# Values as seven products of quarters between the convolution's units, and attention in full f32

## The chip, the cores and the metric

The kernel runs on one core of one Trainium2 chip. The metric is the device time of one execution in microseconds (us). Three executions before the change took 316.39, 316.88 and 317.06 us, with a median of 316.88.

The core's engines work side by side, each through its own queue, in order: TensorE (PE) multiplies matrices, VectorE (DVE) and ScalarE (ACT) work element by element, GpSimd (POOL) does small things and issues some transfers, and SyncE (SP) issues most transfers.

## What is computed

One decoder layer on 256 tokens of width 1024, with two mixers that read the same modulated, normalised input `h`:

```python
proj = h @ w_in
q, k, v, g_attn, cb, cc, cx, g_conv, m_attn, m_conv = jnp.split(proj, IN_OFFSETS, axis=-1)
attn = moba_attention(split_heads(q), split_heads(k), split_heads(v), rel_bias)
y_attn = (attn * jax.nn.silu(g_attn)) @ w_o_attn
y_conv = (short_conv(cb, cc, cx, conv_w) * jax.nn.silu(g_conv)) @ w_o_conv
merged = jax.nn.sigmoid(m_attn) * y_attn + jax.nn.sigmoid(m_conv) * y_conv
return x + gate[:, None, :] * (merged @ w_out)
```

With 256 tokens there is one block of keys, so the attention is plain causal attention of 8 heads of 128 with a bias by distance. A final RMSNorm follows. All data are float32.

## The kernel before

**Two halves for one number.** PE is fast in a reduced-precision form of float32 (`F32R`). The kernel splits each operand into a high half in that form, made by ACT (`split`, L75), and a low half, the rest, made by DVE (L76). A product is then three: high by high, low by high, high by low. Full-f32 products are written with plain f32 operands and need no split.

**Stages.** The transposed normalised input lies in `xnT`. In the first stage Q and K are built up in all eight PSUM banks, over eight k-tiles (`passes`, L205), while the modulated input `H` is made in halves k-tile by k-tile; the full value of a k-tile, `hf`, stands in a small buffer of its own (`full_h`). Then `evac` copies the eight banks into `QK`; ACT and DVE share that, and the splits of the first two weights of the next stage stand between (`vsplit`).

**V** comes next, as one block: `rows_half` makes each 512-column half of V from two weight quarters of 512 x 512 for both halves of the tokens. With two halves of the width, two of the depth and two of the tokens that is eight blocks of twelve PE products (four k-tiles, three products each, 512 columns).

**Units.** Then come twelve units of the convolution mixer: for `j` in 0 to 3 a `cc`, a `cx` and a `cb` unit, after them four `gc` and four `ga` units (the SiLU gates). A unit (`unit`, L350) loads 1 MB of weights through SP, splits them and makes 256 columns of the projection: 16 products of 512 columns (L358) and 16 of 256 (L360), then a `fold` on ACT and DVE.

**Slots.** The attention of head pairs 0 to 3 is spread over numbered slots, one behind each unit: `att_prep` splits Q and K of the pair, `att_scores` (slots 0, 3, 6, 9) makes the scores and the softmax, `att_trans` (slots 3, 6, 9, 12) transposes the weights and splits them and V, `att_out` (slots 6, 9, 12, 13) multiplies. A pair's transposes thus stand three slots behind its scores. Behind each `cx` unit, `gate_part` reduces 1 MB of weights on DVE for the layer's gate.

**Seven products.** `mc` and `oc`, the merge gate's projection and the convolution's output projection, are already made by the class `Seven`: the 1024 x 1024 weight and the input are cut in quarters, and seven products of quarters with sums of quarters replace eight. The sums of weights are made by transfers that add into their target (`add_on`, on POOL's queue); the sums of inputs are made by `combos`, which adds the halves of its input back together and forms four differences in buffers of their own. `p1` to `p7` are the products, interleaved with `ga` and `ma` (`tile`) units.

**Order.** The order of each engine's queue is made at compile time by a scheduler, from the program's order and from when it reckons an instruction's inputs to be ready. Instructions in `pin(...)` keep the program's order among themselves. Buffers: raw weights go round in five 1 MB buffers, and the halves in three each. PSUM banks are handed out in a ring.

Of the kernel before, what the change touches and what calls it, by code (L numbers as in the profile page):

```python
# [17 lines left out]
P = 128  # L18
D = 1024
# [21 lines left out]
def layer_kernel(ctx: ExitStack, tc, x, c, vec, wp_all, slab_all, onehot, final_g, out):  # L41
# [9 lines left out]
    RAW_BUFS = 5  # L51
# [9 lines left out]
    def raw_tile(shape, name):  # L61
        return wp.tile(shape, F32, tag="raw", name=name, bufs=RAW_BUFS)
# [24 lines left out]
    csb, cs = wide[:, 0:D], wide[:, D:D + P]  # L87
# [182 lines left out]
    hfs[0] = tp.tile([P, S], F32, tag="low", name="hf0", bufs=4)  # L270
# [13 lines left out]
    pin(nc.gpsimd.dma_start(rvd, rv))  # L284

# [64 lines left out]
    def unit(key, rhs, dst):  # L350
        name = f"{key[0]}{key[1]}"
        raw = load(key, "w" + name).rearrange("p (k n) -> p k n", k=KT)
        hi, lo = split(raw, [P, KT, 256], name)
# [23 lines left out]
    def rows_half(blk, n, xs, ready=None):  # L377
        a = [bank(f"a{blk}{n}{t}") for t in range(2)]
        for kh in range(2):
            if ready:  # L380
                hi, lo = ready[kh]
            else:
                raw = load((blk, n, kh), f"w{blk}{n}{kh}").rearrange("p (k n) -> p k n", k=4)
                hi, lo = split(raw, [P, 4, 512], f"{blk}{n}{kh}")
            for t in range(2):
                rows_mm(a[t], xs, t, hi, lo, 4 * kh, slice(0, 512), kh == 0, kh == 1)
        return a

    for n in range(2):
        av = rows_half("v", n, H, None if n else v0)  # L390
        for t in range(2):
            nc.scalar.activation(V[:, t, 512 * n:512 * (n + 1)], av[t], AF.Copy)  # L392
# [8 lines left out]
    AT = big.tile([P, NH, S], F32, tag="AT", name="AT")  # L401
    softmax, weights = {}, {}

    AX = big.tile([P, 3, 1536], F32R, tag="GA", name="AX")

    def hi_lo(i, c0, w, a):

        return [AX[:, i, c0 + s * a * w:c0 + (s + 1) * a * w].rearrange("p (a w) -> p a w", a=a) for s in range(2)]

    def put_halves(dst, src):  # L410
        hi, lo = dst
        nc.scalar.activation(hi, src, AF.Copy)
        nc.vector.tensor_sub(lo, src, hi.bitcast(F32))
# [4 lines left out]
    def att_prep(i):  # L418
        qk = QK.rearrange("p (h a) b -> p h (a b)", a=2)[:, 2 * i:2 * i + 2, P:]
        put_halves(hi_lo(i % 2, 0, 3 * P, 2), qk)  # L420

    def att_scores(i):
        his, los = hi_lo(i % 2, 0, 3 * P, 2)
# [3 lines left out]
        for g in range(2):  # L427
            (qh, kh), (ql, kl) = ((t[:, g, 0:P], t[:, g, P:]) for t in (his, los))
            for j, (q, k) in enumerate(((qh, kh), (qh, kl), (ql, kh))):
                nc.tensor.matmul(pS[g][:, P:384], q, k, start=(j == 0), stop=(j == 2))  # L430
# [17 lines left out]
    def att_trans(i):  # L448
        put_halves(hi_lo(2, 0, S, 1), V[:, 0:1, 2 * i * P:2 * (i + 1) * P])
        ET = tp.tile([P, 2, P], F32, tag="ET", name=f"ET{i}", bufs=1)  # L450
        pT = [bank(f"pT{h}") for h in heads_of(i)]
        for g in range(2):
            for b in range(3):
                cols = slice(b * P, (b + 1) * P)
                nc.tensor.transpose(pT[g][:, cols], softmax[i][:, g, cols], ident)
        his, los = hi_lo(2, 2 * S, S, 2)
        for g in range(2):
            put_halves((his[:, g], los[:, g]), pT[g][:, 0:S])
            nc.scalar.activation(ET[:, g], pT[g][:, S:384], AF.Copy)
        weights[i] = ET  # L460

    def att_out(i):
        pO = bank(f"pO{i}")
        (vh, vl), (eh, el) = hi_lo(2, 0, S, 1), hi_lo(2, 2 * S, S, 2)
        for g in range(2):
            cols = slice(g * P, (g + 1) * P)
            for j, (v, e) in enumerate(((vh, eh), (vh, el), (vl, eh))):
                pin(nc.tensor.matmul(pO[:, g * S:(g + 1) * S], v[:, 0, cols], e[:, g], start=(g == j == 0),
                                     stop=False, skip_group_check=True))
        for g, h in enumerate(heads_of(i)):  # L470
            pin(nc.tensor.matmul(pO[:, g * S + P:(g + 1) * S], V[:, 1, h * P:(h + 1) * P], weights[i][:, g],
                                 start=False, stop=(g == 1), skip_group_check=True))
# [3 lines left out]
    slots = [[] for _ in range(14)]  # L476
# [9 lines left out]

    n = 0
    for j in range(4):
        cc = unit(("cc", j), H, tmp("cc", f"cc{j}"))
        run_slot(n)  # L490
        n += 1
        cx = unit(("cx", j), H, tmp("cx", f"cx{j}"))
        run_slot(n)
# [34 lines left out]

    def add_on(t, key):
        pin(nc.gpsimd.dma_start(t, wp_all[UNIT[key]], accum_op=ALU.add))  # L530

    def combos(x, name, tags):
# [21 lines left out]
        return {3: out[0], 1: out[1], 2: out[3], 4: out[4]}  # L554

    class Seven:
        def __init__(self, blk, x, sink, home):
            self.blk, self.x, self.sink, self.home = blk, x, sink, home
# [4 lines left out]
        def begin(self):  # L563
            self.sum = big.tile([P, 2048], F32, tag=self.home, name=self.blk + "sum")
# [3 lines left out]
        def begin_first(self):  # L568
            self.first = load(self.key(1, 2), self.blk + "t1")
            add_on(self.first, self.key(1, 1))  # L570

        def product(self, a, raw, name, start, s=0, t=0, kh=0):
            hi, lo = split(raw.rearrange("p (k n) -> p k n", k=4), [P, 4, 512], self.blk + name)
            for k in range(4):
                if s:
                    xh, xl = self.sx[s][:, k, 0:P], self.sx[s][:, k, P:]
                else:
                    xh = self.x[:, 4 * kh + k, t * P:(t + 1) * P]
                    xl = self.x[:, 4 * kh + k, S + t * P:S + (t + 1) * P]
                for i, (w, xp) in enumerate(((hi, xh), (lo, xh), (hi, xl))):  # L580
                    nc.tensor.matmul(a, xp, w[:, k], start=(start and k == i == 0), stop=(k == 3 and i == 2),  # L581
                                     skip_group_check=True)
# [324 lines left out]
```

## Time and profile before

| what | value |
|---|---|
| median of three executions | 316.88 us (316.39 to 317.06) |
| span of the profiled execution, first to last instruction | 314.8 us |
| mean granted PE clock | 0.999 |
| end of Q/K, start of V on PE | 58.32 us |
| start of the first `cc` unit | 80.10 us |
| start of the first `ga` unit | 181.49 us |
| start of the `oc` product p5 | 247.38 us |
| data moved by transfers | 81.13 MB, 258 GB/s over the span |

The profile gives the profiled execution's span and not its own total, so the span is set beside the median: 2.1 us lie outside it. Times in rows are from the start of the span. A row of the chain of waits gives start, duration, and what worked; the groups give busy time and the mean duration of one instruction; in the timeline a bracket at the end gives how long the engine had been idle and what ended that.

### The profile page before, as it was taken

Reading aid. Unit: us, or ns where it says so; the run is one execution under the profiler, and the core shown is the slowest. Engines: PE = TensorE matmul, PEld = TensorE weight load, DVE = VectorE, ACT = ScalarE, POOL = GpSimd, SP = SyncE. Lnnn points to the kernel's source line nnn. Section 1 sums busy time; section 2 is a strip of 40 time slices with the busy share of each in tenths; the row PEclk is TensorE's granted clock in tenths of the full one; section 3 lists DMA queues with packets and bytes.
Section 4 is the critical chain, followed back from the end, with each engine's and each line's share of the span. In section 5 each row is a group of like instructions: output and inputs, shape, how many; then the busy total and the mean of one; then the engine's idle time right before and its main releaser. Section 6 shows DMA issues by size and latency. Waiting matters only on the chain.

```text
span 314.8 us, 4582 instructions
## 1 busy us (share of the span) xinstructions
PE 306.3 (97%) x1766; PEld 270.2 (86%) x1766; DVE 263.6 (84%) x343; ACT 200.1 (64%) x287; POOL 13.9 (4%) x26
## 2 busy tenths in 40 slices
PE   7899999999999999999999999999999999999993
PEld 6899999888888989889899888888888888888882
DVE  3998995968597999698778878999998588999943
ACT  2765656954559595666967677688896645653421
POOL 3300000000000000020000100020001000000001
PEclk9999999999999999999999999999999999999999
DMA  7999999987667393959964795859969987730003
GB/s 265 414 410 409 406 414 416 403 348 290 254 239 286 134 327 131 372 147 228 304 232 134 269 244 188 322 129 275 314 232 298 391 280 287 250 131 0 0 2 133
DMA packets 15643, 81.13 MB, mean 258 GB/s; under 512 B 1686, under 2 KB 3206, under 8 KB 8454
## 3 DMA queue, kind: packets, MB, share of 16 engines
q1 hardware_dynamic: 12976, 70.59, 58.4%
q0 software_dynamic: 1328, 8.93, 12.7%
q10 hardware_dynamic: 1318, 1.33, 1.3%
q8 instruction: 14, 0.23, 0.3%
q14 instruction: 7, 0.06, 0.0%
HBM read 79.77 MB, written 1.06 MB: 257 GB/s over the span
## 4 chain that ended last, share of the span: by engine, by line
PE 95%; DMA 2%; DVE 1%; issue 1%; SPq 0%; POOLq 0%; POOL 0%; DVEq 0%
PE acc L205 15%; PE agc L358 5%; PE acb L358 5%; PE acx L358 5%; PE acc L358 5%; PE aga L358 5%; PE mcB L581 3%; PE ocB L581 3%; PE aga L360 2%; PE acb L360 2%; PE acx L360 2%; PE acc L360 2%; PE agc L360 2%; PE aoa L373 2%; PE aoa L374 2%; PE av L374 2%
## 5 line engine op out<-in xcount | busy, mean ns | idle before, releaser
L399 DVE CUSTOM_DVE_ANT_0 gate<-gate,wide,vT 128x1024 f32<-128x1024 f32 x8 | 10.1, 1278 | 0.3 <-DMA gate<-in_wp_dram 0.3
L168 DVE CUSTOM_DVE_ANT_0 ada<-ada,wide,msc 128x1024 f32<-128x1024 f32 x7 | 9.4, 1342 | 0.0
L168 DVE CUSTOM_DVE_ANT_0 ada<-ada,wide,vT 128x1024 f32<-128x1024 f32 x7 | 9.0, 1279 | 0.0
L441 ACT ACTIVATE L<-L,mx 128x128 f32<-128x128 f32 (+1 forms) x16 | 7.1, 443 | 1.2 <-DVE mx L439 1.2
L344 ACT ACTIVATE lowcx<-acx 128x256 f32<-128x256 f32 x8 | 3.0, 376 | 7.2 <-PE acx L360 7.2
L445 ACT ACTIVATE L<-L,rr 128x128 f32<-128x128 f32 (+1 forms) x16 | 5.9, 447 | 0.2 <-DVE rr L443 0.2
L392 ACT ACTIVATE V<-av 128x512 f32<-128x512 f32 x4 | 2.4, 599 | 5.4 <-PE av L375 5.4
L565 POOL DMA_DIRECT2D mcsum<-in_wp_dram x1 | 0.6, 581 | 116.3 <-DVE cx L345 116.3
L76 DVE TENSOR_TENSOR cb0l<-wcb,cb0h 128x2048 fp32r<-128x2048 f32 x1 | 2.3, 2293 | 3.6 <-ACT cb0h L75 3.6
L365 ACT ACTIVATE M<-pm 128x512 fp32r<-128x512 f32 x4 | 2.2, 595 | 4.4 <-PE pm L734 4.4
L76 DVE TENSOR_TENSOR ocp1l<-woc,ocp1h 128x2048 fp32r<-128x2048 f32 x1 | 2.3, 2293 | 3.1 <-ACT ocp1h L75 3.1
L148 PE MATMUL wt<-ones 128*128 128x128 f32 x18 | 3.8, 381 | 1.0 <-DVE ones L134 1.0
L437 DVE CUSTOM_DVE_ANT_0 L<-pS,BI 128x128 f32<-128x128 f32 (+1 forms) x16 | 4.7, 350 | 0.0
L499 DVE SCALAR_TENSOR_TENSOR y<-cc,vT,y 128x255 f32<-128x255 f32 x8 | 3.5, 481 | 1.4 <-ACT y L498 1.4
L344 ACT ACTIVATE lowgc<-agc 128x256 f32<-128x256 f32 x8 | 3.0, 373 | 2.7 <-PE agc L360 2.7
L721 DVE TENSOR_TENSOR wo<-wo,gf 128x2048 f32<-128x2048 f32 x2 | 4.6, 2283 | 0.0
L344 ACT ACTIVATE lowcc<-acc 128x256 f32<-128x256 f32 x8 | 3.0, 371 | 2.3 <-PE acc L360 2.3
L172 ACT ACTIVATE H<-xnT,scs 128x256 fp32r<-128x256 f32 x7 | 4.1, 592 | 0.3 <-DVE scs L168 0.3
L76 DVE TENSOR_TENSOR cc0l<-wcc,cc0h 128x2048 fp32r<-128x2048 f32 x1 | 2.3, 2291 | 2.4 <-ACT cc0h L75 2.4
L148 PEld LDWEIGHTS wt<-ones 128*128 128x128 f32 x18 | 3.4, 284 | 1.0 <-DVE ones L134 1.0
L193 ACT ACTIVATE slab3h<-slab 128x1024 fp32r<-128x1024 f32 x2 | 2.1, 1061 | 3.3 <-DMA slab<-in_slab_dram 3.3
L443 DVE RECIPROCAL rr<-mx 128x4 f32<-128x4 f32 x4 | 0.7, 176 | 4.2 <-ACT L L441 4.2
(548 smaller groups left out, 1119.2 us busy)
## 6 DMA issues: line engine op xcount, KB each, us to landing
ada<-in_wp_dram SPq DMA_DIRECT2D x16, 512.0 KB, 10.3
slab<-in_slab_dram SPq DMA_DIRECT2D x16, 512.0 KB, 10.3
wv<-in_wp_dram SPq DMA_DIRECT2D x4, 1024.0 KB, 11.7
wcc<-in_wp_dram SPq DMA_DIRECT2D x4, 1024.0 KB, 4.9
wcx<-in_wp_dram SPq DMA_DIRECT2D x4, 1024.0 KB, 5.2
gate<-in_wp_dram SPq DMA_DIRECT2D x4, 1024.0 KB, 7.0
wcb<-in_wp_dram SPq DMA_DIRECT2D x4, 1024.0 KB, 6.3
wgc<-in_wp_dram SPq DMA_DIRECT2D x4, 1024.0 KB, 9.0
```

Source lines behind the costliest of these rows:

```text
L76: pin(nc.vector.tensor_sub(lo[:, s], raw[:, s], hi[:, s].bitcast(F32)))
L148: pin(nc.tensor.matmul(wt[:, 0:P], ones, ones, start=True, stop=True))
L168: pin(nc.vector.tensor_tensor_reduce(src, src, csb, vT[:, i:i + 1] if s else 1.0, bias(i, s), ALU.mult, ALU.add, scs[:, i, s:s + 1]))
L205: pin(nc.tensor.matmul(acc[j // 2][:, (j % 2) * S:(j % 2 + 1) * S], w[i][:, j * P:(j + 1) * P], x, start=(i == 0 and j // 2 not in opened) ...
L344: nc.scalar.activation(low, a[:, S:], AF.Copy)
L358: nc.tensor.matmul(a, hi[:, k, cols], rhs[:, k, :], start=(k == 0), stop=False)
L360: nc.tensor.matmul(a[:, S:], lo[:, k, cols], rhs[:, k, 0:S], start=False, stop=(k == KT - 1))
L373: nc.tensor.matmul(a, xh, hi[:, k4, cols], start=(first and k4 == 0), stop=False, skip_group_check=True)
L374: nc.tensor.matmul(a, xh, lo[:, k4, cols], start=False, stop=False, skip_group_check=True)
L399: nc.vector.tensor_tensor_reduce(src, src, csb, 1.0, vT[:, 24 + d:25 + d], ALU.mult, ALU.add, gcol[:, d:d + 1])
L441: nc.scalar.activation(E[:, g, cols], E[:, g, cols], AF.Exp, bias=mx[:, 4 + j:5 + j], accum_out=mx[:, 8 + j:9 + j])
L581: nc.tensor.matmul(a, xp, w[:, k], start=(start and k == i == 0), stop=(k == 3 and i == 2), skip_group_check=True)
```

## The change

1. The eight blocks of V become seven products `v1` to `v7`, in the manner of `Seven`. They no longer stand as a block: behind the units of slots 1 to 6 stand v1; v5; v3; v6; v7 and v2; v4. They use PSUM banks 5 to 7, and the units and the attention of that time the other five.
2. The full value of each k-tile of the modulated input is now written back into `xnT`, so that `combine(xnT)` can form the four differences in place, on DVE, ahead of the first eviction of Q/K. `combo_halves` splits them into halves, once for V and once more for `mc`; the `combos` of `H` is gone. The two splits between the evictions are now those of the first `cc` and `cx` units.
3. V's sums of weights: one addition on DVE, and three adding transfers on POOL's queue.
4. The attention products that were split in halves are now full f32: per head one 256-column score product in place of three, one 256-column output product in place of three. `att_prep` and the splits of the softmax weights and of V are gone, the transposed weights are copied whole by ACT.
5. The attention moves: scores of pairs 0 to 3 to slots 4, 7, 9, 11, transposes to 6, 8, 10, 12, output products to 8, 9, 11, 13. The four gate reductions move to the last two `cx` and the last two `gc` units.
6. Buffers: five named raw buffers; one holds the attention's bias, and one is held from v3 to v7. `Seven` gets its tiles from outside; the first of the `mc` and `oc` sums is now loaded on POOL's queue too, and `oc`'s takes the place of two `mc` combinations. `mc`'s p3 and p4 change places. The vector for the reductions and the products' spare buffers share one tile (`quads`).

The core of the diff:

```diff
     def full_h(i):
-        hfs[i] = tp.tile([P, S], F32, tag="low", name=f"hf{i}", bufs=4)
+        hfs[i] = xnT[:, i, :]
         modulated(i, hfs[i])
...
-    v0 = []
+    def quarter(f, t, kh):
+        return f[:, 4 * kh:4 * kh + 4, t * P:(t + 1) * P]
+
+    def combine(f):
+        f00, f01, f10, f11 = (quarter(f, t, kh) for t in range(2) for kh in range(2))
+        pin(nc.vector.tensor_sub(f11, f10, f11))
+        pin(nc.vector.tensor_sub(f10, f00, f10))
+        pin(nc.vector.tensor_sub(f00, f11, f00))
+        pin(nc.vector.tensor_add(f01, f00, f01))
...
+    combine(xnT)
+    vsum = big.tile([P, 2048], F32, tag="W2", name="vsum")
     for j in range(NT // 2):
-        if j < 2:
-            evac(j, j == 0)
-            v0.append(vsplit(j))
-        else:
-            evac(j, j % 2 == 1)
-    BI = big.tile([P, NH, 256], F32, tag="BI", name="BI")
+        evac(j, j in (0, 3, 5, 7))
+        if j == 0:
+            first_split(0)
+        elif j == 1:
+            first_split(1)
+    raw = load(("v", 0, 0), "wv11")
+    nc.sync.dma_start(vsum, wp_all[UNIT["v", 1, 0]])
+    first_v = {"vp1": split(raw.rearrange("p (k n) -> p k n", k=4), [P, 4, 512], "vp1", 1, pin)}
+    VX = big.tile([P, 4, 4, S], F32R, tag="GA", name="VX")
+    vsx = combo_halves(xnT, [(1, VX[:, 0])], pin)
+    pin(nc.vector.tensor_add(vsum, vsum, raw))
+    raw_ring.remove(4)
+    BI = raw_tile([P, NH, 256], "BI", 4)
...
-    for n in range(2):
-        av = rows_half("v", n, H, None if n else v0)
-        for t in range(2):
-            nc.scalar.activation(V[:, t, 512 * n:512 * (n + 1)], av[t], AF.Copy)
+    def v1():
+        product(vb[0], None, "vp1", own(H, 0, 0), True)
+        nc.scalar.activation(VQ[:, 1], vb[0], AF.Copy)
+
+    def v5():
+        product(vb[2], vsum, "vp5", vsx[1], True)
+        nc.scalar.activation(VQ[:, 0], vb[2], AF.Copy)
+        add_on(vsum, ("v", 1, 1))
+        vsx.update(combo_halves(xnT, [(4, VX[:, 1])]))
...
+    def v6():
+        product(vb[1], vsum, "vp6", vsx[2], True)
+        add_on(vsum, ("v", 0, 1))
+        nc.vector.tensor_add(VQ[:, 2], vb[1], VQ[:, 1])
+        nc.vector.tensor_sub(VQ[:, 0], VQ[:, 0], VQ[:, 1])
+        nc.vector.tensor_sub(v_at(0, 1), vb[2], VQ[:, 2])
+        vsx.update(combo_halves(xnT, [(3, VX[:, 3])]))
+
+    def v7():
+        product(vb[1], held["raw"], "vp7", vsx[3], False)
+        raw_ring.append(held["at"])
+        nc.vector.tensor_sub(v_at(1, 1), VQ[:, 0], vb[1])
+
+    def v2():
+        raw = load(("v", 0, 1), "wv21")
+        product(vb[0], raw, "vp2", own(H, 0, 1), False)
+        nc.scalar.activation(v_at(0, 0), vb[0], AF.Copy)
...
-        for g in range(2):
-            (qh, kh), (ql, kl) = ((t[:, g, 0:P], t[:, g, P:]) for t in (his, los))
-            for j, (q, k) in enumerate(((qh, kh), (qh, kl), (ql, kh))):
-                nc.tensor.matmul(pS[g][:, P:384], q, k, start=(j == 0), stop=(j == 2))
+        for a, h in zip(pS, heads_of(i)):
+            nc.tensor.matmul(a[:, P:384], QK[:, 2 * h, P:], QK[:, 2 * h + 1, :], start=True, stop=True)
...
-        his, los = hi_lo(2, 2 * S, S, 2)
         for g in range(2):
-            put_halves((his[:, g], los[:, g]), pT[g][:, 0:S])
-            nc.scalar.activation(ET[:, g], pT[g][:, S:384], AF.Copy)
+            nc.scalar.activation(ET[:, g], pT[g][:, 0:384], AF.Copy)
...
-        slots[max(3 * i - 2, 0)].append((att_prep, i))
-        slots[3 * i].append((att_scores, i))
-        slots[3 * i + 3].append((att_trans, i))
-        slots[13 if 2 * i + 2 == NH else 3 * i + 6].append((att_out, i))
+        slots[(4, 7, 9, 11)[i]].append((att_scores, i))
+        slots[(6, 8, 10, 12)[i]].append((att_trans, i))
+        slots[(8, 9, 11, 13)[i]].append((att_out, i))
+    early = {1: [v1], 2: [v5], 3: [v3], 4: [v6], 5: [v7, v2], 6: [v4]}
...
-        gate_part(j)
+        if j in (2, 3):
+            gate_part({2: 0, 3: 1}[j])
...
-        def begin_first(self):
-            self.first = load(self.key(1, 2), self.blk + "t1")
+        def begin_first(self, t):
+            self.first = t
+            pin(nc.gpsimd.dma_start(t, wp_all[UNIT[self.key(1, 2)]]))
             add_on(self.first, self.key(1, 1))
...
     tile("ma", 0, 0)
+    mc.p3()
+    oc.begin_first(big.tile([P, 2 * D], F32, tag="V", name="ocfirst"))
+    tile("ma", 0, 1)
     mc.p4()
-    oc.begin_first()
-    tile("ma", 0, 1)
-    mc.p3()
+    raw_ring.remove("BI")
     oc.sx = combos(GC, "c", ("W2", "BI"))
```

More of the change, by code (lines that the diff above doesn't have):

```diff
@@ L351, in unit @@
         name = f"{key[0]}{key[1]}"
-        raw = load(key, "w" + name).rearrange("p (k n) -> p k n", k=KT)
-        hi, lo = split(raw, [P, KT, 256], name)
+        if first:
+            hi, lo = first.pop(0)
+        else:
+            raw = load(key, "w" + name).rearrange("p (k n) -> p k n", k=KT)
+            hi, lo = split(raw, [P, KT, 256], name)
         for t in range(2):
@@ L389, in layer_kernel, with product @@
-    for n in range(2):
-        av = rows_half("v", n, H, None if n else v0)
-        for t in range(2):
-            nc.scalar.activation(V[:, t, 512 * n:512 * (n + 1)], av[t], AF.Copy)
+    def product(a, raw, name, xs, start):
+        hi, lo = first_v.get(name) or split(raw.rearrange("p (k n) -> p k n", k=4), [P, 4, 512], name)
+        for k in range(4):
+            xh, xl = (v[:, k, :] for v in xs)
+            for i, (w, xp) in enumerate(((hi, xh), (lo, xh), (hi, xl))):
+                nc.tensor.matmul(a, xp, w[:, k], start=(start and k == i == 0), stop=(k == 3 and i == 2),
+                                 skip_group_check=True)
@@ new lines, in layer_kernel, with v3 @@
+    held = {}
+    def v3():
+        held["raw"] = load(("v", 1, 1), "wv22")
+        held["at"] = raw_ring.pop()
+        product(vb[2], held["raw"], "vp3", vsx[4], False)
+        add_on(held["raw"], ("v", 1, 0))
+        vsx.update(combo_halves(xnT, [(2, VX[:, 2])]))
+    def v6():
[5 more added lines that the diff above has]
+        vsx.update(combo_halves(xnT, [(3, VX[:, 3])]))
@@ L485, in run_slot, with run_early @@
             f(h)
+    def run_early(i):
+        for f in early.get(i, ()):
+            f()
     n = 0
+    ring[:] = range(5)
+    turn[0] = 0
     for j in range(4):
+        if j == 3:
+            ring[:] = range(8)
+            turn[0] = 2
         cc = unit(("cc", j), H, tmp("cc", f"cc{j}"))
+        run_early(n)
+        if n == 6:
+            AT = big.tile([P, NH, S], F32, tag="AT", name="AT")
         run_slot(n)
@@ L553, in combos, with __init__, begin @@
         combo(4, nc.vector.tensor_add, v2, quarter(0, 1), "cx")
-        return {3: out[0], 1: out[1], 2: out[3], 4: out[4]}
+        return {s: (out[i][:, :, 0:P], out[i][:, :, P:]) for s, i in ((3, 0), (1, 1), (2, 3), (4, 4))}
+    turn3 = [0]
     class Seven:
-        def __init__(self, blk, x, sink, home):
-            self.blk, self.x, self.sink, self.home = blk, x, sink, home
+        def __init__(self, blk, x, sink):
+            self.blk, self.x, self.sink = blk, x, sink
         def key(self, r, c):
             return (self.blk, c - 1, r - 1)
-        def begin(self):
-            self.sum = big.tile([P, 2048], F32, tag=self.home, name=self.blk + "sum")
+        def begin(self, t):
+            self.sum = t
             pin(nc.gpsimd.dma_start(self.sum, wp_all[UNIT[self.key(1, 2)]]))
             add_on(self.sum, self.key(2, 2))
-        def begin_first(self):
-            self.first = load(self.key(1, 2), self.blk + "t1")
+        def begin_first(self, t):
+            self.first = t
+            pin(nc.gpsimd.dma_start(t, wp_all[UNIT[self.key(1, 2)]]))
             add_on(self.first, self.key(1, 1))
         def product(self, a, raw, name, start, s=0, t=0, kh=0):
[L573 to L582, printed above, removed]
+            product(a, raw, self.blk + name, self.sx[s] if s else own(self.x, t, kh), start)
         def quad(self, name):
-            return tp.tile([P, 512], F32, tag="q", name=self.blk + name, bufs=3)
+            turn3[0] += 1
+            c0 = turn3[0] % 3 * 512
+            return quads[:, c0:c0 + 512]
         def kept(self, a, name):
@@ L678, in layer_kernel @@
     mc.p5()
-    oc.begin()
+    raw_ring.append(mc.slot)
+    oc.begin(raw_tile([P, 2 * D], "ocsum", 4))
     gated("ga", AT, GA, 2)
```

121 lines of the change are left out of this document (66 added, 55 removed).

## The prediction

> **What bounds the kernel now.** I read the page's busy shares first, then the busy time by stage, then the chain that ended last, and went to the timeline only for single durations.
>
> ```profile
> PE 306.3 (97%) x1766; PEld 270.2 (86%) x1766; DVE 263.6 (84%) x343; ACT 200.1 (64%) x287; POOL 13.9 (4%) x26
> ```
> ```profile
> 58.32:80.10 21.78, 21.78 (x97) 18.01 (x97) 17.01 (x16) 11.76 (x12) 0.00 (x0) 1.00 0.86 342
> 80.10:156.04 75.94, 75.94 (x464) 67.93 (x463) 64.26 (x119) 54.66 (x112) 2.38 (x3) 1.00 0.70 240
> 156.04:181.49 25.45, 25.45 (x156) 22.73 (x156) 21.48 (x31) 18.27 (x30) 0.86 (x1) 1.00 0.63 212
> 181.49:247.38 65.89, 65.89 (x321) 55.70 (x321) 58.77 (x53) 49.88 (x54) 3.18 (x4) 1.00 0.84 258
> 247.38:307.50 60.12, 60.12 (x291) 50.48 (x290) 50.93 (x47) 29.91 (x29) 1.14 (x2) 1.00 0.42 153
> 99.00:117.00 18.00, 18.00 (x111) 16.12 (x110) 17.28 (x34) 13.73 (x31) 0.00 (x0) 1.00 0.56 200
> ```
> In each stage row the length stands first, then busy time of PE, weight loads, DVE, ACT and POOL, the granted clock, and the DMA share. In every stage the change can reach, PE's busy time equals the length, at a clock of 1.00: there is no bubble to remove, so only PE work taken away can shorten the kernel, and any late operand lengthens it at once. The last row shows how near the next engine is: DVE was busy 17.28 of 18.00 us there, and PE still did not wait.
>
> The span is 314.8 us and the median of the three times 316.88, so 2.1 us lie outside the span. The sum is made against the span and carried over to the median with that 2.1.
>
> **The change part by part.**
>
> *Values on PE.* The stage row 58.32:80.10 is the whole old V stage: 21.78 us for eight blocks of twelve 512-column products. The new V has seven.
>
> ```profile
> 239.22 2.72 PE ocB L581 x12
> 156.04 1.84 PE agc L358 x8
> 157.88 0.95 PE agc L360 x8
> 85.66 0.45 PE pS L426 x4
> 86.11 0.71 PE pS L430 x6
> 122.14 0.72 PE pO L468 x6
> 122.86 0.45 PE pO L471 x4
> ```
> These are rows of the chain: start, duration, work, count. A product of this form takes 2.72 us, so seven take 19.04 and **2.74 us go**. (One half of a unit is 1.84 + 0.95, so a unit is 5.58 us; I use that below.)
>
> *Attention on PE.* Per pair of heads the scores were 0.45 (two full-f32 128-column products, four records) + 0.71 (six reduced-precision 256-column products). The six become two full-f32 256-column products, that is four records. The only such form in the trace is the first block of Q/K:
>
> ```profile
> 11.40 3.72 PE L205 MATMUL acc<-hf,slab 128*128 128x256 f32 x16
> 14.78 2.26 PE L205 MATMUL acc<-H,slab0h 128*128 128x256 f32 x16
> ```
> Sixteen records fill 11.40 to 14.78: 0.211 us each. Four make 0.84, so scores gain 0.13 us; in the output product 0.72 becomes 0.84, plus 0.12. Four pairs: **+1.0 us**. Bounds: if 256 columns cost twice the 128-column record of 0.1125 (0.45/4), four make 0.90 and the sum is +1.5; downwards I allow a record of 0.20, since PE may have paused once in that stretch, which gives +0.7. I take 1.0, the row of the same form. The transposes stay as they are. Net on PE: 1.0 - 2.74 = **-1.74 us** (-1.2 to -2.0).
>
> The Trainium skill, "FP8 and Floating Point Precision", section "TensorE Precision Notes", says that true FP32 takes four passes through the array. By four passes of 0.118 the attention would cost +1.9 us and not 1.0; the row above, 0.42 us for a 256-column product, is below four times 0.118 = 0.47.
>
> *Where Q/K hands over.* The four in-place combinations are queued on DVE ahead of the first eviction.
>
> ```profile
> 50.94 1.23 DVE L200 TENSOR_TENSOR slab7l<-slab,slab7h 128x1024 fp32r<-128x1024 f32 x1 [0.40 <-ACT slab7h L193]
> 54.75 0.69 DVE L324 TENSOR_SCALAR QK<-acc 128x512 f32<-128x512 f32 x1 [2.59 <-PE acc L205]
> 58.15 0.40 PE L373 MATMUL av<-v00h,H 128*128 128x512 f32 x1
> ```
> DVE was idle 2.59 us before that eviction. Four operations of 128x512 (0.69 by the eviction's row, 0.60 apart when queued) take 2.4 to 2.8, so the eviction slips 0.2 us at most. PE wants that bank at 58.15, with 2.7 us to spare: cost 0. The two splits behind it are those that stood there before, of other weights.
>
> *DVE in the V window.* This is the cover that could run out. The old V ran as one block in which DVE was 17.01 of 21.78 busy; the new one stands between seven units and one pair of scores, 7 x 5.58 + 7 x 2.72 + 1.29 = 59.4 us of PE.
>
> ```profile
> L76 DVE TENSOR_TENSOR cb0l<-wcb,cb0h 128x2048 fp32r<-128x2048 f32 x1 | 2.3, 2293 | 3.6 <-ACT cb0h L75 3.6
> L366 DVE TENSOR_TENSOR GC<-sgc,GC 128x512 fp32r<-128x512 f32 x4 | 2.7, 687 | 0.0
> L345 DVE TENSOR_TENSOR gc<-agc,lowgc 128x256 f32<-128x256 f32 x8 | 3.3, 417 | 0.0
> L499 DVE SCALAR_TENSOR_TENSOR y<-cc,vT,y 128x255 f32<-128x255 f32 x8 | 3.5, 481 | 1.4 <-ACT y L498 1.4
> L437 DVE CUSTOM_DVE_ANT_0 L<-pS,BI 128x128 f32<-128x128 f32 (+1 forms) x16 | 4.7, 350 | 0.0
> ```
> DVE must do seven units at 2.29 + 2 x 0.42 (21.9), seven product splits (16.0), the sum of two weight quarters (2.3), four low halves and five value sums at 0.69 (6.2), two rounds of the convolution at 2 x 0.69 + 4 x 0.48 (6.6), the first scores (4 x 0.35 and two small ones, some 1.8), and three evictions (2.1), less the first split, done before 58.3: some 54.6 of 59.4, or 92%. The gate reductions leave this window, which makes it fit. At 96% PE did not wait in the row 99.00:117.00, so I put this at 0; the place most at risk is slot 5, where two products stand side by side (5.44 us of PE) just behind scores. Bound: 0 to 3 us, about one split and its queue. Over the stretch up to the gates' end DVE loses the halves of Q, K, E and V and the sum and differences of H, and gains splits: nearly even.
>
> *Transfers.* Three accumulating loads of V and the first load of the two "first" sums move to POOL's queue, which is nearly empty. Of the V ones each follows a product's split and is used two slots later: at least two units and a product, 13.9 us, lie between, against some 9 for the transfer and 4 for the split. The tight one is that of `oc`: it used to be loaded by SP long ahead; now its tile is the place that the `mc` combinations leave, so it waits for p3, which is moved to p4's old place.
>
> ```profile
> 222.90 2.72 PE mcB L581 x12
> 247.38 2.72 PE ocC L581 x12
> 258.26 2.72 PE ocB L581 x12
> ```
> ```profile
> 198.43 0.57 POOL L565 DMA_DIRECT2D ocsum<-in_wp_dram  x1 [18.05 <-PE mcC L581]
> 207.25 0.86 POOL L530 DMA_DIRECT2D ocsum<-in_wp_dram  x1 [8.25 <-DMA ocsum<-in_wp_dram]
> 207.94 1.06 POOL L530 DMA_DIRECT2D oct<-in_wp_dram  x1
> 239.31 1.92 ACT L75 ACTIVATE ocp5h<-oct 128x2048 fp32r<-128x2048 f32 x1 [1.92 <-PE ama L375]
> ```
> ```profile
> ocsum<-in_wp_dram POOLq DMA_DIRECT2D x3, 1024.0 KB, 8.9
> oct<-in_wp_dram POOLq DMA_DIRECT2D x1, 1024.0 KB, 15.7
> ```
> p3 ends at 225.62 - 1.74 = 223.9. The plain load takes 0.57 + 8.25, the accumulating one 8.9 from issue, so it lands at 241.6; ACT's half of the split (1.92) and DVE's (2.29) end at 245.8. PE wants the low half at 247.38 - 1.74 + 0.23 = 245.9. Nothing is left over for a busy ACT or DVE: I cost **+0.4 us** (0 if both are free, 2 if each is in the middle of a split). Behind it on POOL stands the next accumulation into the `oc` sum. Two accumulations that were queued together landed 207.94 + 15.7 - (207.25 + 8.9) = 7.5 us apart, so this one lands near 249.1 and is split by 253.3, ahead of p6 at 258.26 - 1.74 = 256.5.
>
> The Trainium skill, "DMA: Bandwidth & Descriptors", section "Anatomy of one DMA — SWDGE (gpsimd) path", gives 2.0 us plus bytes at 436 GB/s, 4.4 us for 1 MB (an estimate from that page). The trace has 8.25 and 8.9; by the page's figure this wait would be 0.
>
> *Raw buffers.* One of five goes to the bias for the attention's length, and one is held between v3 and v7. SP waited for buffers before without PE noticing; cost 0, bound 1 us.
>
> **Sum:** -1.74 + 0.4 = **-1.3 us**, 315.6.
>
> **The rivals.**
>
> *1. The transposes wait for softmax (slower).* Scores used to stand three slots ahead of their transposes. Now for pairs 1, 2 and 3 what stands between is 5.58 + 1.29, 5.58 and 5.58 us.
>
> ```profile
> 124.41 0.71 PE pS L430 x6
> 133.13 1.49 ACT L445 ACTIVATE L<-L,rr 128x128 f32<-128x128 f32 x4
> 144.15 0.71 PE pS L430 x6
> 152.63 1.48 ACT L445 ACTIVATE L<-L,rr 128x128 f32<-128x128 f32 x4
> ```
> Softmax took 134.6 - 125.1 = 9.5 and 154.1 - 144.9 = 9.2 us. If PE's queue holds program order, it stands for 2.6 + 3.8 + 3.8 = 10 us and the time is 326. From a wait of 1.3 us in all it eats the gain, so an eighth of this is enough to decide. For it: nothing else hides a transpose at the head of PE's queue. Against it: the order on each engine is made by readiness, and PE's queue shows it where a sum was late:
>
> ```profile
> 275.83 1.28 DVE L708 TENSOR_TENSOR SA<-SA,SC 128x512 f32<-128x512 f32 x2
> 276.46 0.40 PE L373 MATMUL aoa<-oa10h,GA 128*128 128x512 f32 x1
> 276.69 0.38 PE L734 MATMUL pm<-ident,SA 128*128 128x128 f32 x2
> ```
> The transposes of the merged rows, written ahead of `oa10`, were put between its products, at the moment when DVE's first sum was ready, without idle PE. Also DVE and ACT have less to do around the scores than they had. I expect the same there; a partial miss of one third gives 319.
>
> *2. DVE starves PE in the V window.* Row for: 92% and two adjacent products; row against: 96% without a wait. Price 2 to 3 us, which gives 317.6 to 318.6.
>
> *3. Only the handovers cost.* The late `oc` sum at its bound of 2 us or a few small waits take 1.2 to 2 us of the 1.74: 316.3 to 317.2, no difference to be told.
>
> *4. Full f32 costs four reduced-precision products* (0.47 for 256 columns): +1.9 in place of +1.0, which gives 316.5. The first Q/K block speaks against it.
>
> *5. Nothing is late at all,* or the f32 record is at its lower bound: 314.9 to 315.2.
>
> **How the numbers follow.** Chances: forecast, with the V saving, 1.0 for attention and up to 0.8 of handover, 0.50 (315.2 to 316.2); case 5, 0.08; case 3, 0.16; case 4, 0.04; case 2, 0.08; case 1, 0.14. A measurement of this kernel tells about 0.2% (0.6 us) from no change, so faster is below 316.25: 0.50 + 0.08 = 0.58. Within 0.2%: 0.16 + 0.04 = 0.20. Slower: 0.08 + 0.14 = 0.22. The range reaches from 314.9 to 318.5, which leaves out most of case 1 and little else.
>
> **What would show it.** Right: seven runs of twelve products of 2.72 us; four records of about 0.21 us under the 256-column scores; PE's busy time about 304.6 with no idle time between Q/K and the end; transposes of pairs 1 to 3 standing inside the next unit. Wrong: idle PE ahead of a transpose with ACT's scaled copy as the releaser (case 1); idle PE ahead of v7, v2 or v4 released by a low half (case 2); idle PE ahead of the `oc` product p5 (case 3); records near 0.235 us (case 4). The prediction falls if the order of PE's queue doesn't follow readiness, or if the accumulating loads on POOL take much more than 9 us beside SP's.

## The result, and the profile after

The changed kernel takes **320.64 us** (median of five runs, 317.90 to 320.93) against 316.88 (316.39 to 317.21) before: ratio 1.0098, 95% interval [1.0071, 1.0125], so it is slower. Measured once more on another occasion it took 319.75 (six runs), ratio 1.0091 [1.0068, 1.0114]. The forecast was 315.6 with a range up to 318.5. The profiled execution took 320.76 us with a span of 318.7, so 2.1 us lie outside the span, as before.

First the page of the changed kernel: busy time of PE and the other engines, and the line of the clock granted to PE in 40 equal slices of the span (8 us each).

```profile
PE 309.3 (97%) x1738; PEld 270.5 (85%) x1738; DVE 268.2 (84%) x339; ACT 201.7 (63%) x277; POOL 17.7 (6%) x31
...
PEclk9999999999999999999999999999999799999999
```

PE has fewer instructions than before (1738 for 1766) and yet 3.0 us more busy time. One digit of the clock, the 32nd slice, is a 7. So part of the loss is not waiting but slow work, in one place. Where the time went is read from the starts of the first record of each stage in the timeline (us, the row of differences from the same instants of before):

| stage | before | changed | difference |
|---|---|---|---|
| start to first Q/K product | 11.40 | 11.84 | +0.4 |
| Q/K, V, attention, to `ga0` | 169.93 | 169.12 | -0.8 |
| `ga0` to the first record of `oc` p5 | 65.89 | 66.20 | +0.3 |
| p5 and `oa` 0 0, to p1 | 8.16 | 11.96 | **+3.8** |
| p1 to the end of the span | 59.42 | 59.58 | +0.2 |

The first row wanders: over the twelve profiles of this study it lies between 11.1 and 12.1. The gain of V and attention together, in the second row, is there (-0.8) but is half of the forecast -1.74, and one product, p5, gives back several times as much. This is the timeline of PE at p5 in the changed kernel; in brackets stands the idle time ahead and who ended it:

```profile
247.16 0.49 PE L429 MATMUL ocC<-ocp5h,sxcW 128*128 128x512 f32 x1
249.49 0.79 PE L429 MATMUL ocC<-ocp5l,sxcW 128*128 128x512 f32 x1 [1.83 <-DVE ocp5l L81]
250.08 1.05 PE L429 MATMUL ocC<-ocp5h,sxcW 128*128 128x512 f32 x2
250.93 0.63 PE L429 MATMUL ocC<-ocp5l,sxcW 128*128 128x512 f32 x1
251.36 1.05 PE L429 MATMUL ocC<-ocp5h,sxcW 128*128 128x512 f32 x2
252.21 0.63 PE L429 MATMUL ocC<-ocp5l,sxcW 128*128 128x512 f32 x1
252.64 0.75 PE L429 MATMUL ocC<-ocp5h,sxcW 128*128 128x512 f32 x2
253.23 0.39 PE L429 MATMUL ocC<-ocp5l,sxcW 128*128 128x512 f32 x1
253.46 0.39 PE L429 MATMUL ocC<-ocp5h,sxcW 128*128 128x512 f32 x1
```

Twelve records of this product take 2.72 us, 0.227 each, when nothing is late. Here the second came 2.33 us after the first, 2.1 late; and the eleven from 249.49 on took until 253.68, 4.19 us in place of 2.50: another 1.7. Together they are the +3.8. The stages by window (length, then busy time of PE, weight loads, DVE, ACT and POOL, granted clock, DMA share, and last the GB/s moved) put the 1.7 on the clock:

```profile
181.00:247.00 66.00, 66.00 (x322) 55.57 (x320) 53.47 (x50) 46.52 (x51) 3.72 (x5) 1.00 0.75 231
247.00:256.00 9.00, 7.11 (x24) 5.47 (x24) 7.03 (x4) 7.07 (x7) 0.56 (x1) 0.81 1.02 358
256.00:307.00 51.00, 51.00 (x245) 42.73 (x244) 47.69 (x41) 24.42 (x22) 0.00 (x0) 1.00 0.40 151
```
```profile
249.48:252.89 3.41, 3.40 (x8) 2.73 (x9) 2.93 (x2) 2.68 (x3) 0.56 (x1) 0.50 0.94 328
```
The last row is the stretch of the fall by itself: the clock was at half for 3.41 us, which is 1.7 us of PE work lost.

What was late is read backwards along the queues. POOL, ACT and DVE, from their timelines, then SP's loads beside them and the landing of the accumulating load (the last number of its row in the view of DMA issues):

```profile
225.64 0.57 POOL L647 DMA_DIRECT2D ocfirst<-in_wp_dram  x1 [17.31 <-PE mcC L429]
232.03 0.85 POOL L293 DMA_DIRECT2D ocfirst<-in_wp_dram  x1 [5.82 <-DMA ocfirst<-in_wp_dram]
237.07 0.87 POOL L293 DMA_DIRECT2D ocsum<-in_wp_dram  x1 [4.19 <-DMA woa<-in_wp_dram]
```
```profile
245.19 1.92 ACT L80 ACTIVATE ocp5h<-ocfirst 128x2048 fp32r<-128x2048 f32 x1 [8.61 <-DMA ocfirst<-in_wp_dram]
```
```profile
247.14 2.29 DVE L81 TENSOR_TENSOR ocp5l<-ocfirst,ocp5h 128x2048 fp32r<-128x2048 f32 x1 [7.55 <-ACT ocp5h L80]
```
```profile
223.15 9.42 SPq L71 DMA_DIRECT2D woa<-in_wp_dram  x2
234.01 5.97 SPq L71 DMA_DIRECT2D woc<-in_wp_dram  x2
```
```profile
ocfirst<-in_wp_dram POOLq DMA_DIRECT2D x1, 1024.0 KB, 13.1
```

The plain load of `ocfirst` was issued at 225.64 when p3 released the place, 1.7 us later than the 223.9 of the working. It landed sooner than reckoned, so the accumulating one was issued at 232.03, 0.7 us ahead of the working's 232.7. But the accumulating load landed 13.1 us after its issue and not 8.9. ACT stood idle 8.61 us for it and DVE 7.55; both were free, the data were not there. SP issued three loads of 1 MB in those 13 us: at 232.24 and 239.65, the second of each group (start plus length, less the 0.33 of the last issue), and at 234.01.

### The profile page after: what moved, and what is told of

Its sections match the earlier page's. It is cut to its first block, busy times and chain, and to the rows that moved or that the text cites. A ratio compares the mean times of both kernels' runs of the same rounds, so it can differ in the third digit from the quotient of the medians.

```text
span 318.7 us, 4512 instructions
## 1 busy us (share of the span) xinstructions
PE 309.3 (97%) x1738; PEld 270.5 (85%) x1738; DVE 268.2 (84%) x339; ACT 201.7 (63%) x277; POOL 17.7 (6%) x31
## 3 DMA queue, kind: packets, MB, share of 16 engines
q0 software_dynamic: 2048, 14.17, 19.5%
## 4 chain that ended last, share of the span: by engine, by line
PE 83%; DMA 6%; issue 4%; ACT 2%; DVE 2%; POOL 1%; POOLq 0%; DVEq 0%; ACTq 0%
PE acc L211 15%; PE acc L405 5%; PE agc L405 5%; PE acx L405 5%; PE aga L405 5%; DMA ocfirst<-in_wp_dram 4%; PE acb L405 3%; PE acc L407 2%; PE aga L407 2%; PE agc L407 2%; PE aoa L422 2%; PE aoa L421 2%; PE aoa L420 2%; PE ocC L429 2%; DMA gate<-in_wp_dram 2%
## 5 line engine op out<-in xcount | busy, mean ns | idle before, releaser
L487 DVE CUSTOM_DVE_ANT_0 gate<-gate,quads,vT 128x1024 f32<-128x1024 f32 x8 | 10.1, 1277 | 1.8 <-DMA gate<-in_wp_dram 1.8
L174 DVE CUSTOM_DVE_ANT_0 ada<-ada,quads,msc 128x1024 f32<-128x1024 f32 x7 | 9.4, 1342 | 0.0
L174 DVE CUSTOM_DVE_ANT_0 ada<-ada,quads,vT 128x1024 f32<-128x1024 f32 x7 | 9.0, 1281 | 0.0
L81 DVE TENSOR_TENSOR ocp5l<-ocfirst,ocp5h 128x2048 fp32r<-128x2048 f32 x1 | 2.3, 2292 | 7.6 <-ACT ocp5h L80 7.6
L574 ACT ACTIVATE y<-cc,vT 128x256 f32<-128x256 f32 x8 | 3.7, 500 | 2.1 <-DVE cc L570 2.1
L405 PE MATMUL agc<-H,gc1h 128*128 128x512 f32 x16 | 4.8, 413 | 0.0
L388 ACT ACTIVATE lowcb<-acb 128x256 f32<-128x256 f32 x8 | 2.9, 367 | 2.5 <-PE acb L407 2.5
L405 PE MATMUL acb<-H,cb3h 128*128 128x512 f32 x16 | 4.3, 403 | 0.0
L178 ACT ACTIVATE xnT<-xnT,scs 128x256 f32<-128x256 f32 x7 | 4.2, 599 | 0.2
L405 PE MATMUL acc<-H,cc2h 128*128 128x512 f32 x16 | 4.1, 401 | 0.2 <-ACT cc2h L80 0.2
```

Of the source, the lines that this page charges most:

```text
L174: pin(nc.vector.tensor_tensor_reduce(src, src, csb, vT[:, i:i + 1] if s else 1.0, bias(i, s), ALU.mult, ALU.add, scs[:, i, s:s + 1]))
L178: pin(nc.scalar.activation(dst, xnT[:, i, :], AF.Identity, scale=scs[:, i, 1:2], bias=scs[:, i, 0:1]))
L388: nc.scalar.activation(low, a[:, S:], AF.Copy)
L405: nc.tensor.matmul(a, hi[:, k, cols], rhs[:, k, :], start=(k == 0), stop=False)
L487: nc.vector.tensor_tensor_reduce(src, src, csb, 1.0, vT[:, 24 + d:25 + d], ALU.mult, ALU.add, gcol[:, d:d + 1])
```

## The experiments

In the text, *stretch* is the time from the first Q/K product to `ga0`, read as in the table (before 169.93, changed 169.12), and *p5 to p1* the fourth row of it (8.16 and 11.96).

**1. p3 earlier.** The load for p5 is released a tile of 5.4 us earlier.

```
     mc.p2()
-    tile("ma", 0, 0)
     mc.p3()
     oc.begin_first(big.tile([P, 2 * D], F32, tag="V", name="ocfirst"))
+    tile("ma", 0, 0)
     tile("ma", 0, 1)
```

> mc's p3 and the two loads of the oc first sum stand ahead of the first ma unit, so both loads start 5.4 us earlier; no other change. Theory A (the late oc first sum costs some 3.8 us at p5: a wait of 2.1 for its low half and 1.7 of products at a lower clock behind it): PE does not wait at p5, its clock stays 1.00, and the time falls by 3 to 4 us to about 317. Theory B (the loss is spread: full-f32 products and a fuller DVE in the V window): the time stays within 1 us of 320.6.

317.39 us (ten runs), ratio to before 1.0013 [0.9992, 1.0034]. From POOL's timeline and PE's waits in this kernel:

```profile
227.89 0.85 POOL L293 DMA_DIRECT2D ocfirst<-in_wp_dram  x1 [5.38 <-DMA ocfirst<-in_wp_dram]
```
```profile
PE agc L405 <- DVE gc L389: 1.6, 1, 1.6
PE wt L154 <- DVE ones L140: 1.0, 1, 1.0
PE acc L405 <- ACT cc2h L80: 0.4, 1, 0.4
PE ama L421 <- DVE ma10l L81: 0.2, 1, 0.2
```

The load landed 10.9 us after its issue, before PE wanted it; no row of p5 is left among the waits and p5 to p1 is 8.16 again. Between 2.4 and 3.3 us are back (against 319.75 and 320.64), so the late operand at p5 is where the loss was. Smaller waits remain; the profiled execution took 319.0 us, 1.6 more than the median, so its wait of 1.6 us at `gc` is probably not in the median.

**2. The second sum left out.** Another accumulating load stands on POOL's queue right behind. It goes, for `oc`.

```
         def p7(self):
...
-            add_on(self.sum, self.key(1, 1))
+            if self.blk != "oc":
+                add_on(self.sum, self.key(1, 1))
```

> The accumulation into the oc sum behind p7 is left out, so p6 of oc works with one weight quarter too few. It is the transfer that is issued 5 us after the late accumulation of the oc first sum. If the two share the queue's rate, the first sum lands 8 to 9 us after its issue and not 13.1, the wait at p5 falls from 2.1 us to 0 to 0.5 and the time by 2 to 4 us. If SP's two loads of 1 MB beside it are what slows it, it still takes 12 us or more and the time stays.

319.72 us, ratio 1.0088 [1.0056, 1.0120]. The load and the wait are as they were:

```profile
ocfirst<-in_wp_dram POOLq DMA_DIRECT2D x1, 1024.0 KB, 12.7
```
```profile
PE ocC L429 <- DVE ocp5l L81: 1.7, 1, 1.7
```

The load behind it on the same queue is not what slows it: without it 0.4 us less of 13.1.

**3. SP's loads left out.** On the changed kernel, all of SP's weight loads for `oc` and `oa` are left out; the loads of `wo` are tied to places that come free late, so that they do not move up into the gap.

```
-        raw = load((blk, n, kh), f"w{blk}{n}{kh}").rearrange("p (k n) -> p k n", k=4)
+        if blk == "oa":
+            raw = GA[:, 0:4, :].bitcast(F32)
+        else:
+            raw = load((blk, n, kh), f"w{blk}{n}{kh}").rearrange("p (k n) -> p k n", k=4)
...
         def load(self, r, c):
+            if self.blk == "oc":
+                return GA[:, 0:4, :].bitcast(F32).rearrange("p k n -> p (k n)")
...
+    raw_ring[:] = [4, "BI"]
```

> The changed kernel with all of SP's weight loads of oc and oa left out (their products read the tile GA in place of the weights, so the outputs are not the reference's), so that nothing of SP's moves beside the accumulating load for oc p5. Theory A (the accumulating load shares the DMA engines with SP's loads, which took it from 8.9 to 13 us): it lands 8 to 9 us after its issue, PE has no wait at p5, and the time is 2 to 4 us below the changed kernel: 316.5 to 318.5. Rival (an accumulating load queued behind a plain one with the second sum behind it takes 13 us by itself): it still takes over 12 us and PE waits 1.8 us as before.

316.49 us, ratio to before 0.9987 [0.9974, 0.9999], 3.3 us under the changed kernel's second measurement and 4.2 under its first. Landing, and ACT's half of the split:

```profile
ocfirst<-in_wp_dram POOLq DMA_DIRECT2D x1, 1024.0 KB, 7.9
```
```profile
238.47 1.92 ACT L80 ACTIVATE ocp5h<-ocfirst 128x2048 fp32r<-128x2048 f32 x1 [2.65 <-DMA ocfirst<-in_wp_dram]
```

With nothing of SP's beside it, and with the second sum still behind it, the same load on the same queue lands in 7.9 us: SP's loads beside it are the cause, shown from both sides. PE has no wait after the first Q/K product, and p5 to p1 is 8.16. The Trainium skill, "DMA: Bandwidth & Descriptors", section "Queues, rings and completion order", says that each DMA engine takes turns between the queues that have work, a packet at a time; 7.9 us alone and 13 beside SP agree with that. The fit in its section "Anatomy of one DMA — SWDGE (gpsimd) path", 4.4 us for 1 MB by an estimate from it, is below both.

**4. The wait filled.** Nine full-f32 products of the constant `ones` into the bank of p5, ahead of it, which p5's own first product clears.

```
         def p5(self):
             self.c = bank(self.blk + "C", 2)
+            if self.blk == "oc":
+                for _ in range(9):
+                    nc.tensor.matmul(self.c[:, 0:P], ones, ones, start=True, stop=True)
```

> Nine idle full-f32 products of two constant 128x128 tiles (2.0 us of PE) stand ahead of oc's p5, in the bank that p5 then opens. If the wait of 2 us alone lowered the clock behind it, the products of p5 come every 0.23 us again, and the time falls by 1.2 to 1.7 us although the low half lands no earlier. If the clock falls for another reason (a limit on power, say), the records of p5 stay at 0.43 us and the time stays or rises.

319.57 us, ratio 1.0083 [1.0050, 1.0115]. In the profile PE is hardly idle there (busy 8.92 of 9.00 us) and the clock stays up:

```profile
247.00:256.00 9.00, 8.92 (x47) 7.41 (x46) 8.47 (x4) 6.49 (x5) 0.56 (x1) 1.00 1.00 355
```

By itself this would say that the idle time lowers the clock. But in experiment 2 PE waits 1.7 us, unfilled, and has 1.00 too:

```profile
247.00:256.00 9.00, 7.36 (x32) 6.10 (x33) 8.48 (x5) 6.25 (x5) 0.57 (x1) 1.00 0.63 242
```

So one profile of the filled wait does not settle it, and its median (319.57) is within 0.2 us of that of the unfilled one when measured again (319.75).

**5. The changed kernel again.**

> The changed kernel once more, unaltered, beside e9_p4_back_between on the same chip. Both theories: 319 to 321, a wait of 1.5 to 2 us at oc p5 with the accumulating load landing 12 to 14 us after its issue. If the records behind the wait are at their usual spacing here (0.23 us), the stretched ones of the first profile belong to that execution and not to the wait.

319.75 us, as above. The wait is there, the accumulating load landed after 13.0 us, and the clock behind the wait fell in this profile too:

```profile
248.88 0.50 PE L429 MATMUL ocC<-ocp5l,sxcW 128*128 128x512 f32 x1 [1.82 <-DVE ocp5l L81]
```
```profile
247.00:256.00 9.00, 7.18 (x25) 5.73 (x25) 7.27 (x4) 6.47 (x5) 0.56 (x1) 0.81 1.00 360
```

p5 to p1 is 12.00. So the stretched records don't belong to the first profiled execution alone: two of two profiles of this kernel have them (here the clock is at 0.50 from 249.89 to 253.30), and the profiled executions of experiments 2 and 6, with a wait as long, do not. The mean clock of every execution is on record too; it is a coarse sign, since the clock of the very first and last microseconds counts in it. Where the wait was left empty (both measurements of the changed kernel and experiment 2, 21 executions) it was 0.993 or less in 8, and these took 320.07 to 322.50 us; the other 13 took 317.90 to 321.73. Where there was no wait at p5 (experiments 1, 3, the first of 7, and 9; 42 executions) or a filled one (4), it never fell below 0.994. This speaks for the empty wait as what brings the fall, in some executions of a kernel and not in others; for the filled wait, four executions are few.

**6. The gate column's loads later.** DVE waited in the changed kernel for a load of the gate column, on its in-order queue, and PE felt it at `cc2`:

```profile
105.08 1.28 DVE L487 CUSTOM_DVE_ANT_0 gate<-gate,quads,vT 128x1024 f32<-128x1024 f32 x1 [1.01 <-DMA gate<-in_wp_dram]
...
110.12 3.06 PE L405 MATMUL acc<-H,cc2h 128*128 128x512 f32 x12 [0.16 <-ACT cc2h L80]
```

Tried on the changed kernel: the four parts at `cb3`, `gc1`, `gc2`, `gc3`.

```
-        if j in (2, 3):
-            gate_part({2: 0, 3: 1}[j])
+        if j == 3:
+            gate_part(0)
...
-        if j in (2, 3):
-            gate_part({2: 2, 3: 3}[j])
+        if j >= 1:
+            gate_part(j)
```

> The first gate reduction moves from slot 8 to the last cb unit, the second from there to the second gc unit; the others stay. Theory A: DVE stood 1.0 us for that gate's load, with the softmax's reciprocal behind it, then ACT's copies and the split of cc2: without it the unit cc2 takes 5.6 us and not 6.3, and the time falls by 0.7 us. Theory B (two products side by side are too fast for the splits whatever else is queued): the unit stays at 6.2 or more, and the time too.

325.97 us, ratio 1.0268 [1.0222, 1.0314]: no theory had this. The timeline of DVE, then of PE:

```profile
137.73 1.28 DVE L487 CUSTOM_DVE_ANT_0 gate<-gate,quads,vT 128x1024 f32<-128x1024 f32 x1 [5.47 <-DMA gate<-in_wp_dram]
```
```profile
139.41 2.12 PE L405 MATMUL acc<-H,cc3h 128*128 128x512 f32 x8 [2.96 <-DVE cb L389]
```

Here the reduction held DVE's queue for 5.47 us until its data came, with the sum of `cb` behind it, and PE behind that. The move had put the reduction in front of a sum that PE needed at once.

**7. Loads kept, reductions a unit later; and loads earlier.** Both on experiment 1, which repairs p5. In the first, a part's load stays where it is and its two reductions are written one unit later (part 3's behind `ga0`). In the second, parts 2 and 3 are also loaded ahead of `gc0` and `gc1`.

```
         if j in (2, 3):
-            gate_part({2: 0, 3: 1}[j])
+            gate_load(j - 2)
         cb = unit(("cb", j), H, tmp("cx", f"cb{j}"))
...
+        if j in (2, 3):
+            gate_part(j - 2)
```

> e1_p3_before_ma with the gate column's four loads issued where they are and their reductions on DVE written one unit later (gate 3's behind ga 0). Theory A (DVE's queue stood at a reduction whose load had not landed, and PE waited behind it for the low halves and sums): DVE has no idle time released by a gate load, the waits of 1.6 us in gc and 0.4 in cc2 are gone, and the time is 0.7 to 1.8 us below that of e1_p3_before_ma: 315.6 to 316.7. Rival (PE's waits there come from DVE's amount of work, not from the load): no change, 317.4, and the waits stand with another releaser.

> As e6_reductions_a_unit_later, with gate 2 and gate 3 loaded ahead of gc 0 and gc 1 (two units earlier) and reduced behind gc 1 and gc 2. Theory A: as there, 315.6 to 316.7, with no wait at ga 0 either. Rival (the gate loads and reductions are 10.2 us of DVE's work and 4 MB in any place, and collide with softmax and the halves of gc): 317.4 or more.

The first took 317.27 us, ratio 1.0009 [0.9998, 1.0019]: against 1.0013 in experiment 1 no difference can be told, although the wait at `gc` is gone from its profile. But the edit hardly moved anything: in DVE's timeline all eight reductions stand where they stood in experiment 1, behind the same instructions (the scheduler orders by readiness), and the first, at 104.80, still has DVE idle for 1.12 us ahead of it, with PE waiting 0.3 us at `cc2`. So this run is close to a second measurement of experiment 1 and does not test its expectation; the 0.7 to 1.8 us had been read from one profiled execution. The second took 323.04, ratio 1.0204 [1.0187, 1.0220]. That is within the rival's "317.4 or more", but not for the rival's reason (DVE's amount of work): it is the mechanism of experiment 6 again,

```profile
133.94 1.28 DVE L492 CUSTOM_DVE_ANT_0 gate<-gate,quads,vT 128x1024 f32<-128x1024 f32 x1 [3.86 <-DMA gate<-in_wp_dram]
```
```profile
136.42 3.18 PE L405 MATMUL acc<-H,cc3h 128*128 128x512 f32 x8 [3.55 <-DVE cb L389]
```

Behind this wait, too, the clock was at 0.50 for 3.41 us (137.16 to 140.57); in experiment 6's profile, behind 2.96 us, it was not.

**8. Full-f32 attention alone.** The kernel before, with the scores and output products in full f32 and no halves made for them; slots, V and `oc` as before.

```
-        for g in range(2):
-            (qh, kh), (ql, kl) = ((t[:, g, 0:P], t[:, g, P:]) for t in (his, los))
-            for j, (q, k) in enumerate(((qh, kh), (qh, kl), (ql, kh))):
-                nc.tensor.matmul(pS[g][:, P:384], q, k, start=(j == 0), stop=(j == 2))
+        for a, h in zip(pS, heads_of(i)):
+            nc.tensor.matmul(a[:, P:384], QK[:, 2 * h, P:], QK[:, 2 * h + 1, :], start=True, stop=True)
```

> The kernel before with one part of the change alone: attention products in full f32 (no halves made by ACT and DVE), the scores, transposes and output products in their old slots, V as before. Theory A (PE sets the time, two records per full f32 product at 0.217 us each): +0.15 us per pair of scores and +0.14 us per pair of output products, +1.2 us in all, 318.1 us, ratio about 1.004. Theory B (what ACT and DVE no longer do pays for it): 316.9 or less. If it is over 319, the full f32 products cost more in time than their records show.

318.19 us, ratio 1.0040 [1.0025, 1.0055], which is +1.1 to +1.2; its stretch is 171.12, +1.19. Theory A holds: what ACT and DVE no longer do pays nothing.

**9. The best order found.** The first of experiment 7 with p4 set back between the two tiles.

```
     oc.begin_first(big.tile([P, 2 * D], F32, tag="V", name="ocfirst"))
     tile("ma", 0, 0)
+    mc.p4()
     tile("ma", 0, 1)
-    mc.p4()
```

> e6_reductions_a_unit_later with mc p4 set back between the two tiles ma 0 (p2, p3, ma 0 0, p4, ma 0 1), so that DVE's sum and half for p4 no longer stand right ahead of the half for ma 1 0. Theory A (PE's 0.2 us wait and the slow record at ma 1 0, 0.5 us in all from ga 0 to oc p5, come from that order): no wait there, 316.4 to 317.0, at most 0.2% below the kernel before. Rival (the loads of this stretch are late, whatever the order): 317.3 as before. Neither expects a time below 316.

316.60 us (eleven runs), ratio to before 0.9993 [0.9982, 1.0005]. All of PE's waits that its profile shows lie ahead of the first Q/K product:

```profile
PE px L218 <- DVE xx L261: 1.9, 1, 1.9
PE wt L154 <- DVE ones L140: 1.0, 1, 1.0
PE px L218 <- ACT xx L258: 0.3, 1, 0.3
```

Its stretch is 168.65 and p5 to p1 8.16. The time and the missing wait are as Theory A had them, but against experiment 7's first run (1.0009 [0.9998, 1.0019]) the intervals overlap, so the gain from p4's place is not shown. It is about 1% faster than the changed kernel, and can't be told from the kernel before. Not tried: V in seven products with the attention as it was, since the combinations of V and the attention's halves take the same tile.

## Why the prediction was wrong

**The step that failed** is the one headed *Transfers*: the accumulating load of `oc`'s first sum, sized at 8.9 us from issue and so costed at +0.4 us, 2 at most. Its chain of steps was right (p3 frees the place, plain load, accumulating load, two halves of the split, p5), and the working said that nothing was left over. The load took 13.1 us, 4.2 too many. Three smaller errors together took half of that back: the plain load was issued 1.7 us later than reckoned, it ended 2.4 us sooner after its issue, and PE came to p5 1.5 us later, so 2.1 us of delay were left. The row of 8.9 was of an accumulating load beside which SP issued one load (at 208.79); here there were three. Experiments 2 and 3 together show that it is SP's traffic that counts: 12.7 us without the queue's next load, 7.9 without SP's loads. Two more accumulating loads, the first in the kernel before and the second in the changed one, show what the number of loads tells and what not:

```profile
236.41 0.86 POOL L530 DMA_DIRECT2D ocsum<-in_wp_dram  x1 [27.41 <-DVE ocp7l L76]
```
```profile
ocsum<-in_wp_dram POOLq DMA_DIRECT2D x1, 1024.0 KB, 9.3
```
```profile
121.87 0.87 POOL L293 DMA_DIRECT2D mcsum<-in_wp_dram  x1 [5.85 <-DMA mcsum<-in_wp_dram]
```
```profile
mcsum<-in_wp_dram POOLq DMA_DIRECT2D x1, 1024.0 KB, 12.6
```

The second has three loads of SP's beside it, the first of them issued 1.6 us behind it, and took nearly as long as that of p5. The first has two, at 240.15 and 243.58, and one still running that was issued at 233.67, and took only 9.3. So the count alone does not give the time, and what does is left open. The prediction named a slow load beside SP's as what would bring it down ("if the accumulating loads on POOL take much more than 9 us beside SP's"), but neither range nor chances paid for it: the bound of 2 us allowed for a busy ACT or DVE and took the transfer as known.

**The size of a wait on PE** was a second error in the same step. A low half that is 2.1 us late cost 2.1; what was added in the profiled executions, 1.7 us of records at half pace, no term and no rival had. Rival 3, "the late `oc` sum at its bound", is the case that came, at twice its bound, and so on the other side of no change.

**V in seven products.** The forecast was -2.74 on PE. The sum of the intervals between PE's records is 21.79 us for the old V and 19.21 in experiments 3 and 9: -2.58, nearly as forecast. In the changed kernel's profiled run it is 19.5.

**Full f32** was costed at +1.0 (0.7 to 1.5) from a record of 0.211; it measures +1.19 in experiment 8, within the bounds. The chain's rows of a pair in the changed kernel, scores 0.87 and outputs 0.86 for four records, give the 0.217 of that expectation, 0.15 and 0.14 us more a pair. The rival of four reduced-precision passes, +1.9, is out.

**Together** these two give -1.39 and a stretch without any wait shows -1.20 (experiment 3) or -1.28 (experiment 9), where -1.74 was forecast; the last 0.1 to 0.2 us were not taken apart further. Even with no wait at p5 the forecast of 315.6 was not reached: experiments 3 and 9 took 316.49 and 316.60, which is 0.6 and 0.4 below the kernel before as measured beside them. Where the rest of the stretch's gain went is left open.

**DVE in the V window** was costed at 0, with 0 to 3 as its bounds. In the two profiles of the changed kernel the stretch is 169.12 and 168.94, 0.3 to 0.5 us over that of experiment 9. The chain leads through the gate column's load at `cc2`, and not to slot 5, where the working saw the risk; that DVE's queue stood for a load, and not for work, no step had. Five profiles with this order bear it out: with DVE idle 0.64 (experiment 9), 0.74 (the changed kernel again), 1.01 (changed), 1.12 (first of 7) and 1.27 us (experiment 1) for that load, PE waited 0, 0, 0.16, 0.26 and 0.40 at `cc2`.

**The transposes and softmax** (the rival on the slow side, with the largest price) cost nothing that a profile shows, and for the reason given: the queue holds the order of readiness. PE's timeline in the changed kernel has the transposes of one pair in two places inside the unit `cb3`, without idle time:

```profile
147.62 0.60 PE L523 MATMUL pT<-ident,L 128*128 128x128 f32 x4
147.99 0.47 PE L405 MATMUL acb<-H,cb3h 128*128 128x512 f32 x1
148.30 0.42 PE L523 MATMUL pT<-ident,L 128*128 128x128 f32 x2
148.48 1.86 PE L405 MATMUL acb<-H,cb3h 128*128 128x512 f32 x7
```

**The cover behind Q/K** held: 46.75 us of that stage before and after.

## What to carry to other kernels

Time a transfer from a row with the same neighbours, not only of the same kind and size: list what the other queues issue between its issue and its landing, and where a move leaves no slack, price the wait with a slower transfer too: here one took 13 us where the row had 9. Where PE fills the whole span, one operand a few us late can cost more than a saving on PE brings (here 3.8 us against 1.3), so ask of every buffer that changes hands when its last reader ends and when its next load can start. On an in-order queue a short instruction whose load is late holds all behind it, so moving such a load to a place that looks emptier can cost more than it saves. And where a scheduler sets the order, look in the trace whether an edit moved anything before reading its time.

## What the runs showed of the hardware

- **Clock behind a wait.** With 1.8 us of idle PE ahead, the granted clock fell to one half for 3.41 us in two of two profiles of the changed kernel (records 0.43 us apart, nearly twice 0.227), and behind 3.55 us in the second of experiment 7; in the profiles of experiments 2 and 6, after waits of 1.7, 1.8 and 2.96 us, it stayed at 1.00. The mean clock was 0.993 or less in 8 of 21 executions with the empty wait of some 2 us, and in none of 46 without it; what decides between executions is left open. The Trainium skill, "TensorE: Matmul & The Clock Gate", section "Part 1: The HAM clock gate (the "warmup" mystery)", has PE fall to half its clock after at least one idle window of about 3.4 us, and says that the window runs free of the kernel. The half pace and its varying from profile to profile fit that; here less than 2.4 us between two records was enough.
- **Accumulating loads of 1 MB** took 7.9 us with nothing of SP's beside them, and 12.6 and 13.1 with three of SP's loads issued beside them; one with two issued beside it and a third still running took 9.3.
- **A full-f32 product of 256 columns** takes 0.43 us in the attention (two records of 0.217), a little more than the 0.42 of the first Q/K block.
